# Rounding two of five stored parts into tiles of the results' pool

## The chip, the cores and the metric

The kernel runs on one core of one Trainium2 chip, as one launch. The metric is the device time of one execution, in microseconds (us). Before the change three executions took 2423.63, 2425.55 and 2424.79 us; the median is 2424.79 us. A measurement of this kernel can tell a difference of about 0.2% (some 4.8 us) from none.

## The reference, cut to what matters

One layer of a decoder on 512 tokens of width 2048, all in float32:

```
h = rmsnorm(x, g_mix);  z = h @ w_in            # conv, attention and gate columns
merged = gc * (conv_y @ w_conv_out) + ga * (attn @ w_attn_out)
x = x + merged @ w_mix_out                       # the mixing projection
h = rmsnorm(x, g_mlp)                            # the second norm
u = square(relu(h @ w_ff1));  x = x + u @ w_ff2  # the MLP
out = rmsnorm(x, g_final)
```

The change touches the rows between the mixing projection and the first MLP product: the projection's results, transposed and scaled, are combined into the sums that the MLP's first product reads.

## The kernel before, in words

**Products.** Every large product is done by Winograd's form of Strassen's scheme: a 2x2 block product with seven products instead of eight, named A11, A12, S1, S2, S3, S4 and A22 after the combination of the left operand that they use. `Group` does one such set of seven for 512 columns of weights. Each weight quarter is a 1 MB tile `x`, loaded by a transfer on SP's queue. Since TensorE works in a rounded float32 here, each operand is split in two: ScalarE (ACT) rounds it into `th` (`high_of`, line 111) and VectorE (DVE) subtracts that to get the rest, `tl` (`low_of`, line 114). A product is then three passes over the same PSUM bank: high by high, high by low, low by high. `th` and `tl` have two buffers each, so a split can start only when TensorE has done with the `th` of two products earlier. In the mixing projection one product is 48 matmuls (`mm_rows`, lines 187, 189 and 191: 16 with `th` and 8 with `tl` for each of two blocks of tokens).

**The mixing projection** is four groups, g = 0 to 3. For each group, `Mix(g)` takes the four result blocks (`put`, line 1266: adds the residual x and stores to `x1_d`). `turn` squares them for the norm (line 524), transposes them on TensorE (line 1283, into `ptr`) and copies the transposes into two tiles `f` (line 1292). Then `sums` makes the five combinations S1, S2, S3, S4 and A22 that the MLP's left operand needs, and `out` splits each in high and low and sends both to `h_d` in HBM by a transfer from GpSimd's (POOL's) queue. This is done for g = 0, 1 and 2, each during the next group's products; A11 and A12 are kept unsplit in `f_d`. Group 3 keeps its parts in the core's memory. After the last group the stored parts are read back (`begin_part`, line 1241).

**The last group** uses `tail3`. Its order of products is A11, A12, S1, S2, S4, S3, A22. The bank `a` holds A11 + S2, is copied and read three times, and is then overwritten by A22. While it runs, the MLP's first group `g0` starts: its weights are loaded from POOL's queue (`x<-in_w_ff`), the stored half of A11 and A12 is split (`split_part`), and its products A11 and A12 follow A22 on TensorE.

**Tiles.** The results of the groups (`o`), the residual rows (`xr`) and a few others come from one tag with five places of 128x512 float32 (`otile`). The rounded parts come from `staged`, a tag with two places. A place is handed out again when everything that reads the old tile is done, the transfer that stores it included. A rounding into a `staged` tile thus waits for the landing of the store of the part two before it.

**Order.** The order on each engine is made by the layer that records the program: it plans with its own estimates, and moves work ahead where it believes another would wait. It is fixed when the program is built; on the chip each engine works through its list strictly in order, so an instruction that waits holds all behind it. `split_in_order` pins the part splits in the order of the program on ACT and DVE.

Of the kernel before, what the change touches and what calls it, by code (L numbers as in the profile page):

```python
# [9 lines left out]
F32R = mybir.dt.float32r  # L10
# [5 lines left out]
P = 128  # L16
# [4 lines left out]
HS = S // 2  # L21
# [23 lines left out]
@with_exitstack  # L45
def tile_hybrid_block(ctx: ExitStack, tc, x, g_mix, w_in, b_f, b_gate, conv_w, w_conv_out,
                      w_attn_out, w_mix_out, g_mlp, w_ff1, w_ff2, g_final, out):
    nc = tc.nc
    x, out = x[0], out[0]
# [20 lines left out]
    def otile(shape, name, dt=F32):  # L70
        return main.tile(shape, dt, tag="o", name=name, bufs=5)
# [44 lines left out]
    def split(src, hi, lo):  # L116
        return high_of(src, hi), low_of(src, hi, lo)
# [3 lines left out]
    def split_in_order(*how, kept=None):  # L121

        for i in split(*how):
            tc.keep_in_program_order(i)
            parted[kept] = i

    def sub(out, a, b):
        return nc.vector.tensor_tensor(out=out, in0=a, in1=b, op=ALU.subtract)  # L128
# [841 lines left out]
    n = 0  # L970
# [244 lines left out]
    def staged():  # L1215
        return pm.tile([P, 2, HS], F32R, tag="staged", name="staged", bufs=2)
# [7 lines left out]
    n = turns[0] + 1  # L1224
# [24 lines left out]
    class Mix:  # L1249
# [50 lines left out]
        def out(self, n, src):  # L1300
            g = self.g
            if self.last:
                split(src, Q2[n][:, 0, 2 * g:], Q2[n][:, 1, 2 * g:])
            else:
                hi = staged()
                split_in_order(src, hi, src)
                for e, o in enumerate((hi.bitcast(F32), src)):
                    nc.gpsimd.dma_start(out=h_d[:, SPLIT.index(n), e, 2 * g:2 * g + 2], in_=o)
# [424 lines left out]
```

## Time and profile before

| | |
|---|---|
| three executions | 2423.63, 2425.55, 2424.79 us |
| span of the profiled execution | 2423.6 us, mean granted TensorE clock 0.998 |
| TensorE (PE) busy | 2401.9 us (99%) |
| VectorE busy | 2041.3 us (84%) |
| ScalarE busy | 1202.6 us (50%) |
| mixing projection's products | to 1188 us; the third group begins near 1106, the last near 1146 us |
| MLP's first product | from about 1188 us |

The profile gives times from the start of the span. In a timeline row stand the start, the duration, the engine, the line, the operation with output and input (buffer numbers left out), shapes, and in brackets the idle time of the engine before it with what ended it. A matmul's duration includes the drain of the pipeline; the distance of two starts is what it costs. The row of a window gives its length, then for PE, PE's weight loads, DVE, ACT and POOL the busy time and, in brackets, the number of instructions, then the granted clock, the share of the transfer engines and GB/s. In a row of transfers the last number is the time from issue to landing.

### The profile page before, as it was taken

The page shows a single profiled execution, that of the slowest core. Times are in us where ns is not written, and L with a number is a line of the kernel's source. Part 1 is how long each engine was busy: PE and PEld are TensorE (multiplying, and loading weights), DVE is VectorE, ACT ScalarE, POOL GpSimd, SP SyncE. Part 2 cuts the span into 40 slices and gives each one's busy share as a digit, 9 for nine tenths or more (in the row PEclk, how much of TensorE's full clock was granted, in tenths as well). Part 3 has the DMA queues.
Part 4 walks back from the last instruction along what each step waited for, and adds up shares of the span by engine and source line. Part 5 has one row for each costly group of instructions (what it writes and reads, how often), then busy time and mean ns, then how long its engine had stood idle before and what let it go on. Part 6 is the DMA issues. An engine that isn't in the chain of part 4 may idle for free.

```text
span 2423.6 us, 41438 instructions
## 1 busy us (share of the span) xinstructions
PE 2401.9 (99%) x17783; PEld 2260.7 (93%) x17783; DVE 2041.3 (84%) x1739; ACT 1202.6 (50%) x1230; POOL 299.9 (12%) x480
## 2 busy tenths in 40 slices
PE   9999999999999999999999999999999999999998
PEld 9999899999999999899999999999998888888886
DVE  7887677788887878898989889898887888889898
ACT  7443434445545534355666566666664333333334
POOL 1110111111111111022300000000011001100000
PEclk9999999999999999999999999999999999999999
DMA  8665454464656755657855564655678567665662
GB/s 276 188 187 153 148 157 140 144 189 152 201 187 199 239 179 187 209 169 243 315 201 207 198 232 177 231 192 200 229 296 291 166 217 251 217 206 184 235 229 101
DMA packets 279847, 491.98 MB, mean 203 GB/s; under 512 B 11820, under 2 KB 191112, under 8 KB 279280
## 3 DMA queue, kind: packets, MB, share of 16 engines
q1 hardware_dynamic: 226384, 272.71, 35.7%
q0 software_dynamic: 52672, 215.57, 24.3%
q8 instruction: 139, 2.28, 0.4%
q10 hardware_dynamic: 608, 1.06, 0.1%
q14 instruction: 44, 0.36, 0.0%
HBM read 379.70 MB, written 109.07 MB: 202 GB/s over the span
## 4 chain that ended last, share of the span: by engine, by line
PE 86%; DVE 4%; issue 4%; DMA 3%; ACT 1%; POOL 1%; SPq 0%; DVEq 0%; POOLq 0%; ACTq 0%
PE a L168 6%; PE a L172 6%; PE a L170 6%; PE a L189 5%; PE a L187 5%; PE a L191 5%; PE d L168 5%; PE d L170 5%; PE d L172 5%; PE c L168 4%; PE c L170 4%; PE c L172 4%; PE d L191 3%; PE d L189 3%; PE d L187 3%
## 5 line engine op out<-in xcount | busy, mean ns | idle before, releaser
L111 ACT ACTIVATE th<-x 128x2048 fp32r<-128x2048 f32 (+1 forms) x280 | 537.0, 1918 | 503.7 <-DVE x L128 159.2
L114 DVE TENSOR_TENSOR tl<-x,th 128x2048 fp32r<-128x2048 f32 (+2 forms) x282 | 639.4, 2273 | 162.1 <-ACT th L111 150.5
L128 DVE TENSOR_TENSOR x<-x,x 128x2048 f32<-128x2048 f32 (+1 forms) x160 | 366.0, 2288 | 24.4 <-DMA x<-in_w_in_dram 18.9
L111 ACT ACTIVATE th<-y 128x2048 fp32r<-128x2048 f32 (+1 forms) x109 | 185.4, 1701 | 273.9 <-PE a L189 138.8
L114 DVE TENSOR_TENSOR tl<-y,th 128x2048 fp32r<-128x2048 f32 (+1 forms) x109 | 219.0, 2014 | 29.3 <-ACT th L111 28.9
L187 PE MATMUL a<-th,us 128*128 128x512 f32 x512 | 199.3, 389 | 0.4 <-ACT th L111 0.4
L189 PE MATMUL a<-th,us 128*128 128x512 f32 x512 | 199.2, 389 | 0.0
L170 PE MATMUL c<-S,th 128*128 128x256 f32 x848 | 196.4, 277 | 0.0
L168 PE MATMUL c<-S,th 128*128 128x256 f32 x848 | 196.3, 277 | 0.0
L168 PE MATMUL a<-S,th 128*128 128x256 f32 x784 | 181.1, 277 | 0.0
L170 PE MATMUL a<-S,th 128*128 128x256 f32 x784 | 180.7, 276 | 0.0
L170 PEld LDWEIGHTS c<-S,th 128*128 128x128 f32 x848 | 159.3, 188 | 0.2 <-issue 0.2
L168 PEld LDWEIGHTS c<-S,th 128*128 128x128 f32 x848 | 159.4, 188 | 0.0
L170 PEld LDWEIGHTS a<-S,th 128*128 128x128 f32 x784 | 147.3, 188 | 0.0
L168 PEld LDWEIGHTS a<-S,th 128*128 128x128 f32 x784 | 147.2, 188 | 0.0
L191 PE MATMUL a<-tl,us 128*128 128x512 f32 x512 | 136.9, 389 | 0.6 <-DVE tl L114 0.6
L170 PE MATMUL b<-A,th 128*128 128x256 f32 x544 | 127.3, 279 | 0.0
L168 PE MATMUL a<-A,th 128*128 128x256 f32 x544 | 126.7, 278 | 0.0
L168 PE MATMUL d<-S,th 128*128 128x256 f32 x544 | 126.1, 277 | 0.0
L170 PE MATMUL a<-A,th 128*128 128x256 f32 x544 | 126.0, 277 | 0.0
L168 PE MATMUL b<-A,th 128*128 128x256 f32 x544 | 126.0, 276 | 0.0
L170 PE MATMUL d<-S,th 128*128 128x256 f32 x544 | 125.7, 277 | 0.0
(398 smaller groups left out, 6065.2 us busy)
## 6 DMA issues: line engine op xcount, KB each, us to landing
x<-in_w_in_dram SPq DMA_DIRECT2D x86, 1024.0 KB, 6.0
y<-in_w_ff_dram SPq DMA_DIRECT2D x64, 1024.0 KB, 7.7
x<-in_w_ff_dram SPq DMA_DIRECT2D x60, 1024.0 KB, 8.6
us<-s_d POOLq DMA_DIRECT2D x48, 1024.0 KB, 9.3
s_d<-rh POOLq DMA_DIRECT2D x32, 896.0 KB, 5.2
s_d<-r POOLq DMA_DIRECT2D x32, 896.0 KB, 6.0
x<-in_w_mix_out_dram SPq DMA_DIRECT2D x17, 1024.0 KB, 6.7
g_d<-o POOLq DMA_DIRECT2D x32, 256.0 KB, 3.1
```

The lines of the kernel that those rows point to most:

```text
L111: return tied(nc.scalar.activation(out=hi, in_=src, func=AF.Copy))
L114: return tied(nc.vector.tensor_tensor(out=lo, in0=src, in1=hi.bitcast(F32), op=ALU.subtract))
L128: return nc.vector.tensor_tensor(out=out, in0=a, in1=b, op=ALU.subtract)
L168: nc.tensor.matmul(o, hi[:, q, js], Sh, start=first and q == 0 and j == 0, stop=False, skip_group_check=True)
L170: nc.tensor.matmul(o, hi[:, q, js], Sl, start=False, stop=False, skip_group_check=True)
L172: nc.tensor.matmul(o, lo[:, q, js], Sh, start=False, stop=q == nq - 1, skip_group_check=True)
L187: tied(nc.tensor.matmul(o, Sh, hi[:, q, :], start=begin and q == 0, stop=False, skip_group_check=True))
L189: tied(nc.tensor.matmul(o, Sl, hi[:, q, :], start=False, stop=False, skip_group_check=True))
L191: tied(nc.tensor.matmul(o, Sh, lo[:, q, :], start=False, stop=q == nq - 1, skip_group_check=True))
```

## The change

In `Mix.out`, for the parts S1 and A22, the rounded half goes into a tile `hi` of the results' tag (five places) and no longer into one of the two `staged` tiles. S2, S4 and S3 stay with `staged`. Nothing is added or removed: the same roundings, subtractions and stores are done, with the same shapes.

```
-                hi = staged()
+                hi = otile([P, 2, HS], "hi", F32R) if n in ("S1", "A22") else staged()
```

A group now takes eight tiles of the five-place tag, not six. In the built program the places fall as follows (numbers are the program's own). In the second group `hi_11634` (S1) takes the place of `o_11346`, and `hi_11832` (A22) that of `o_11406`, both results of the first group; `o_11840` then follows `hi_11634`, and `o_11897` follows `hi_11832`. In the last group `hi_12764` (A22) lies where the result block `o_12827` has to go; before the change `o_12827` followed `o_12555`.

The planner's order moves with it. The first piece is ACT's in the second group, - before and + with the change. `th_11902` is the high half of the weights of that group's last product, A22; `staged` and `hi` are roundings of parts of group 0; `o_11777` is the copy of the bank of S3.

```order
 L111 ACTIVATE th_11845<-x11_11650 128x2048
 L111 ACTIVATE staged_11629<-f_11031 128x512
-L111 ACTIVATE staged_11634<-s1_11619 128x512
+L111 ACTIVATE hi_11634<-s1_11619 128x512
+L111 ACTIVATE staged_11706<-f_11032 128x512
 L260 ACTIVATE o_11777<-d_11712 128x512
-L111 ACTIVATE staged_11706<-f_11032 128x512
-L111 ACTIVATE staged_11832<-f_11032 128x512
+L111 ACTIVATE hi_11832<-f_11032 128x512
 L111 ACTIVATE th_11902<-x10_11538 128x2048
```

S1 and A22 go into `hi`, S3's rounding moves ahead of the copy, and the third and fourth rounding no longer share places with the two before them.

The second piece is ACT's in the last group, from the MLP's first half splits on. `th_12891` belongs to A22 of the mixing projection, `th_12981` to A11 of the MLP, `o_12770` and `o_12827` are the copies of the banks of S2 and S4; `A11_12615` is the stored half of the MLP's A11.

```order
+L1288 ACTIVATE A12_12684<-ptr_12753,cols_97 128x256
+L111 ACTIVATE th_12891<-x10_12461 128x2048
+L1292 ACTIVATE f_12455<-ptr_12753,cols_97 128x256 x2
+L111 ACTIVATE hi_12764<-f_11969 128x512
 L260 ACTIVATE o_12770<-a_12463 128x512
 L111 ACTIVATE A11_12615<-A11_12615 128x1536
-L1288 ACTIVATE A12_12684<-ptr_12753,cols_97 128x256
-L1292 ACTIVATE f_12455<-ptr_12753,cols_97 128x256 x2
-L111 ACTIVATE staged_12764<-f_11969 128x512
+L111 ACTIVATE th_12981<-x00_12822 128x2048
 L260 ACTIVATE o_12827<-c_12629 128x512
-L111 ACTIVATE th_12891<-x10_12461 128x2048
```

The copy `o_12827` now stands behind `th_12981`, and the split of the mixing projection's A22 ahead of the copies. On DVE the addition of bank `a` to `o_12827` (`o_12827<-a_12463`), the last reader of that bank before A22 overwrites it, moved from ahead of `tl_12892` to behind `tl_12982`, the low half that goes with `th_12981`.

The third piece is TensorE's in the last group: the end of S3 (`d_12832`), then A22 of the mixing projection (`a_12463`), its transposes, and A11 of the MLP (`a_12980`). The change's order, without its further rows of the same kind:

```order
 L191 MATMUL d_12832<-tl_12834,M_10785 128x256 x2
 L191 MATMUL d_12832<-tl_12834,M_10986 128x256 x2
+L168 MATMUL a_12980<-A11_12615,th_12981 128x256
+L170 MATMUL a_12980<-A11_12615,th_12981 128x256
...
 L187 MATMUL a_12463<-th_12891,M_10539 128x256
 L189 MATMUL a_12463<-th_12891,M_10539 128x256
...
 L1283 MATMUL ptr_12962<-ident_90,o_12692 128x128 x4
-L168 MATMUL a_12980<-A11_12615,th_12981 128x256
-L170 MATMUL a_12980<-A11_12615,th_12981 128x256
```

28 of the 48 matmuls of the MLP's A11 moved from behind the mixing projection's A22 to ahead of it.

## The prediction

> **What bounds the kernel now.** The page first: engine shares and the chain that ended last.
>
> ```profile
> PE 2401.9 (99%) x17783; PEld 2260.7 (93%) x17783; DVE 2041.3 (84%) x1739; ACT 1202.6 (50%) x1230; POOL 299.9 (12%) x480
> PE 86%; DVE 4%; issue 4%; DMA 3%; ACT 1%; POOL 1%; SPq 0%; DVEq 0%; POOLq 0%; ACTq 0%
> ```
>
> TensorE is busy for 99% of the span, so an edit to roundings on ACT can only be worth what TensorE waits near them. Next, windows over the mixing projection and PE's waits from 1030 to 1230 us:
>
> ```profile
> 1080.00:1100.00 20.00, 17.33 (x143) 16.93 (x142) 12.99 (x12) 10.13 (x13) 6.13 (x11) 0.96 0.90 296
> 1160.00:1180.00 20.00, 18.80 (x166) 18.61 (x165) 18.16 (x20) 14.93 (x23) 9.43 (x16) 1.00 0.81 282
> PE d L187 <- ACT th L111: 2.5, 1, 2.5
> PE c L187 <- ACT o L260: 1.2, 1, 1.2
> ```
>
> Two waits, 2.5 us in the second group and 1.2 us in the last, are all that TensorE loses there, and the first costs it speed as well. The ACT timeline shows what the first comes from, the PE timeline and 1 us windows what it costs:
>
> ```profile
> 1083.27 0.57 POOL L1308 DMA_DIRECT2D h_d<-staged  x1 [6.84 <-ACT staged L111]
> 1086.08 0.63 ACT L111 ACTIVATE staged<-s 128x512 fp32r<-128x512 f32 x1 [0.30 <-DMA h_d<-staged]
> 1094.90 0.63 ACT L111 ACTIVATE staged<-f 128x512 fp32r<-128x512 f32 x1 [7.71 <-DMA h_d<-staged]
> 1096.28 1.89 ACT L111 ACTIVATE th<-x 128x2048 fp32r<-128x2048 f32 x1
> 1098.22 0.58 PE L187 MATMUL d<-th,M 128*128 128x256 f32 x1 [2.53 <-ACT th L111]
> 1105.52 0.60 PE L1283 MATMUL ptr<-ident,o 128*128 128x128 f32 x4
> 1111.41 0.82 PE L1283 MATMUL ptr<-ident,o 128*128 128x128 f32 x6
> 1099.00:1100.00 1.00, 1.00 (x7) 1.00 (x6) 1.00 (x1) 1.00 (x2) 0.00 (x0) 0.50 0.97 377
> 1100.00:1101.00 1.00, 1.00 (x7) 1.00 (x7) 1.00 (x2) 1.00 (x1) 0.00 (x0) 0.50 0.23 90
> ```
>
> ACT stands 7.71 us before a rounding into `staged`, since the store that empties the tile has not landed; behind it queues `th` of A22, and TensorE waits for that. After the wait the granted clock is 0.50, and the pass takes 1105.52 - 1098.22 = 7.30 us; the next takes 1111.41 - 1105.52 less 0.44 for four transposes = 5.45 us. The slow clock costs 1.85 us. The 1.2 us wait leaves the clock at 1.00 and comes from ACT's order (a split and a rounding ahead of a copy), which the change leaves alike.
>
> **The change, part by part.** The work is the same; only places and order move.
>
> *Second group: the 2.5 us wait goes.* S2 and S4 take the two `staged` tiles, S1 a place whose old content was stored a group earlier. S3 follows S2, whose store was issued at 1083.27 and landed 2.7 us later, by the first row below. S4's, issued at 1086.7, took 8.1 us, and that is what ACT waits for now; A22 takes a free place too.
>
> ```profile
> h_d<-staged POOLq DMA_DIRECT2D x1, 256.0 KB, 2.7
> h_d<-staged POOLq DMA_DIRECT2D x1, 256.0 KB, 8.1
> h_d<-f POOLq DMA_DIRECT2D x1, 256.0 KB, 8.4
> 1088.76 1.07 PE L191 MATMUL a<-tl,M 128*128 128x256 f32 x8
> ```
>
> From 1086.0 ACT runs S1, S3, a copy and A22 without a stop to about 1088.0; `th` can start when TensorE has read its buffer's old content (1088.76), and is done near 1090.8, with 4.7 us to spare. What is late next: the copies of the next transposes into `f` (L1292) overwrite a tile whose last store is issued near 1089.0 and took 8.4 us, so they start at 1097.4 and hold up `th` of the third group's first product: 1097.4 + 0.8 + 0.6 + 0.4 + 1.9 = 1101.1. TensorE needs it at 1095.53 + 5.45 + 0.44 = 1101.4. That just holds. **Term A: -2.5 - 1.85 = -4.4 us**; between 0 and -4.4.
>
> *Third group.* Here ACT now does the two copies into `f` and a rounding ahead of `th` of S2, which before came first:
>
> ```profile
> 1125.84 1.93 ACT L111 ACTIVATE th<-x 128x2048 fp32r<-128x2048 f32 x1 [4.15 <-DVE x L128]
> 1127.88 0.84 ACT L1292 ACTIVATE f<-ptr,cols 128x256 f32<-128x256 f32 x2
> 1129.52 0.28 PE L187 MATMUL a<-th,M 128*128 128x256 f32 x1
> h_d<-f POOLq DMA_DIRECT2D x1, 256.0 KB, 4.5
> ```
>
> The copies wait for a store that is issued near 1122.7. If it takes 4.5 us as before, `th` ends at 1127.2 + 0.7 + 0.5 + 1.9 = 1130.3, 0.8 us late; if it takes 2.7 us, `th` ends by 1128.5 and nothing is late. The queue has less in it, so I take nearer the lower end. **Term B: +0.3 us**, between 0 and 0.8.
>
> *Last group: a new wait.* The rows that carry it (PE, ACT, DVE timelines, and the store of A22's rounding, issued at 1177.6):
>
> ```profile
> 1175.62 1.07 PE L191 MATMUL c<-tl,M 128*128 128x256 f32 x8
> 1181.06 1.07 PE L191 MATMUL d<-tl,M 128*128 128x256 f32 x8
> 1181.97 0.28 PE L187 MATMUL a<-th,M 128*128 128x256 f32 x1
> 1183.78 1.07 PE L191 MATMUL a<-tl,M 128*128 128x256 f32 x8
> 1187.01 1.11 PE L191 MATMUL a<-tl,M 128*128 128x256 f32 x8
> 1181.26 1.92 ACT L111 ACTIVATE th<-x 128x2048 fp32r<-128x2048 f32 x1 [0.66 <-PE d L189]
> 1187.21 1.92 ACT L111 ACTIVATE th<-x 128x2048 fp32r<-128x2048 f32 x1
> 1191.26 1.50 ACT L111 ACTIVATE A<-A 128x1536 fp32r<-128x1536 f32 x1
> 1178.11 0.69 DVE L131 TENSOR_TENSOR o<-a,o 128x512 f32<-128x512 f32 x1
> 1192.79 1.76 DVE L114 TENSOR_TENSOR A<-A 128x1536 fp32r<-128x1536 f32 x1 [1.01 <-ACT A L111]
> 1202.07 2.29 DVE L114 TENSOR_TENSOR tl<-x,th 128x2048 fp32r<-128x2048 f32 x1
> 1204.41 2.15 PE L172 MATMUL c<-S,tl 128*128 128x256 f32 x16
> h_d<-staged POOLq DMA_DIRECT2D x1, 256.0 KB, 7.0
> ```
>
> Step 1. After S3's product (its end is the start of the next, 1181.97) TensorE now has 28 matmuls of the MLP's A11. Their `th` is the ACT row at 1181.26; it cannot start before TensorE leaves the same buffer in that S3 product ([0.66 <-PE d]). Done at 1183.2: TensorE waits 1.25 us. Step 2. 16 such matmuls take 1183.78 - 1181.97 = 1.81 us, so 28 take 3.2, to 1186.4. Step 3. A22 then overwrites bank `a`, which DVE must have added to `o_12827` first. That addition ran at 1178.11 and was never near the path. Now ACT's copy that fills `o_12827` waits for `hi_12764`'s store: `th` of A22 can start near 1175.8, then two copies, so the rounding ends near 1179.0; the store lands 7.0 us after, near 1186.0, and the copy is done at 1186.6. On DVE the addition stands behind `tl` of the MLP (2.3 us). That one's turn comes after the subtraction for A22's part, an addition, the low half of A11 (1181.2 to 1182.9, after ACT's high half) and three additions of 0.6 us: 1184.7 to 1186.9. So the addition ends at 1187.6 by either wait. **A22 starts at 1187.65, not 1181.97: 5.7 us later**, 3.2 us of it filled with work brought forward.
>
> Step 4. That work does not come back as a gain. Behind A22's last read of its `th` (1187.01) stands a chain: `th` of the MLP's A12 (1187.21), small copies, the high half of the stored A12 (1191.26), its low half on DVE (1192.79 to 1194.5), then TensorE's A12. TensorE covers it now with A11's 48 matmuls and two sets of transposes. With 28 of them done before, what remains behind A22 is 0.44 + 4 x 0.11 + 1.8 + 0.44 = 3.1 us; the chain still takes 6.6. It slides by the whole 5.7 us, and A12 starts at 1200.15 after a wait of 3.4 us. The DVE chain behind it slides as well (row 1202.07, for which TensorE waits at 1204.41 now). Step 5. A wait of 2.5 us took the clock to 0.50, at a cost of 1.85 us, so one of 3.4 us should: A12 5.45 + 1.85, a small matmul and S1's first 32 matmuls (3.6) end near 1211.2, against DVE's 1204.36 + 5.7 = 1210.05: 1.1 us more. **Term C: +5.7 + 1.1 = +6.8 us.** Its lower bound is 0 (the addition in time, the order harmless), its upper 10: the store takes 10.6 us, as one there did (below), and the chain slides by 3.3 more.
>
> ```profile
> x_d<-o POOLq DMA_DIRECT2D x1, 256.0 KB, 10.6
> ```
>
> The Trainium skill puts this otherwise: its page "TensorE: Matmul & The Clock Gate", section "Part 1: The HAM clock gate", has the clock halved after at least one whole idle window of about 3.4 us. By that rule the 2.5 us wait should have left the clock alone, and this trace differs; a 3.4 us wait would be a toss-up, and without the slow clock the sum would be 1.1 us lower, which the forecast's width holds.
>
> The weight loads of the MLP are issued earlier or at the same time; the read-back of the stored parts follows the last result's store, some 5 us later, but has 10 us and more until its product.
>
> *Sum.* -4.4 + 0.3 + 6.8 = +2.7 us: 2423.6 becomes 2426.3 us in a profiled execution. That one is 1.2 us under the median of the runs, so on the median of 2424.79 I expect **2427.4 us**. Measurement tells 0.2%, 4.85 us, from no change; this is inside.
>
> **The rivals.**
>
> *The wait goes and nothing takes its place.* Term A alone, with C near 0 or 1: 2420.4 to 2421.5 us. For it: A is the largest wait in these stages, and DVE and ACT are not full. Against: the rule that a result follows A22's rounding in its place, and the order in which TensorE meets A11's matmuls first, do not depend on luck. Even in full it stays just under the 4.85 us that counts as faster; it passes that if the 1.2 us wait shrinks too (2419.2).
>
> *Late stores decide, and it is slower.* `o_12827`'s place: if `hi_12764`'s store lands later than 7.3 us after its issue it takes the lead from DVE in step 3, and each us more is a us on the end. At 10.6 us the sum is +6 and the time 2430.8. It sits behind three 1 MB weight loads in POOL's queue, one of which now starts earlier; against it, the store before took 7.0 us in much the same queue.
>
> *The stall moves by one product and does nothing else.* If `f`'s store in term A lands 3 us later, `th` of the third group is late by that, the slow clock returns, and A shrinks to nothing: with C, 2431.9 us. The margin is only 0.4 us, but a delay of 0.5 to 2 us would merely cost its own length.
>
> **How the numbers follow.** My forecast, with steps within 2 to 3 us, has 0.68; the clean gain 0.12; late stores or a stall that moves 0.20. From the first nearly all lies within 0.2% (2420 to 2429.6); of the second a little under half is beyond it, of the third most. That makes 0.06 faster, 0.75 the same, 0.19 slower. The range: the forecast with C 4 us smaller at one end, and late stores at the other, 2422.6 to 2431.0.
>
> **What would show it.** Step A: no wait of PE for `th` near 1095 us, the clock at 1.00 from 1098 to 1102, ACT's roundings of the second group without an idle time over 1 us. Term C: PE idle near 1178 (1182 less 4.4) for `th`, again about 3 us of matmuls later until DVE's `o<-a`, then some 3 us for `A<-A`, with a clock of 0.50 after it. If A22 of the last group starts straight after S3 or A11's 28, or ACT's copy `o_12827` never waits for `h_d<-hi`, step 3 is wrong and the time is that of the first rival; if PE waits at the third group's first product, the margin in A was.

## The result, and the profile after

The changed kernel takes 2432.5 us (median of 7 executions, 2432.0 to 2437.3) against 2425.55 us of the kernel before on the same chip (7 executions, 2421.8 to 2427.2): a ratio of 1.0036 with a 95% interval of 1.0026 to 1.0045. It is slower, by 7 us, where 2.6 us were forecast. The profiled executions differ by 2431.4 - 2423.6 = 7.8 us. Two executions far outside the rest, 9210.5 us of e11 and 4930.7 us of e12, are left out of the ratios below.

The shares of the engines and the chain that ended last, in the page of the changed kernel, say almost nothing: TensorE is as full as before.

```profile
PE 2405.3 (99%) x17783; PEld 2263.2 (93%) x17783; DVE 2041.8 (84%) x1739; ACT 1201.7 (49%) x1230; POOL 299.9 (12%) x480
```

```profile
PE 90%; DVE 3%; issue 3%; DMA 2%; POOL 1%; ACT 1%; SPq 0%; DVEq 0%; POOLq 0%; ACTq 0%
```

TensorE's waits do (waiting engine, tile and line, what it waited for; us in all, times, longest):

```profile
PE ptr L1283 <- DVE o L1266: 3.0, 2, 2.5
PE a L187 <- ACT th L111: 2.2, 1, 2.2
PE b L161 <- ACT A L111: 1.5, 1, 1.5
PE b L170 <- DVE A L114: 1.3, 1, 1.3
PE a L168 <- ACT th L111: 1.1, 1, 1.1
PE c L187 <- ACT o L260: 0.9, 1, 0.9
PE a L187 <- DVE o L131: 0.6, 1, 0.6
PE c L187 <- DVE o L131: 0.5, 1, 0.5
```

The 2.5 us wait for `th` in the second group is gone. In its place stand a wait of transposes for residual additions (3.0), one for an addition to a result (0.5), four in the last group (1.1, 0.6, 1.5, 1.3), and one of 2.2 us that turns out to lie far behind, in the MLP. The wait of 1.2 us for ScalarE's copy is now 0.9. To see where the time went, the same instructions of both kernels are set side by side. TensorE's timeline of the changed kernel, with one row of VectorE's from the MLP:

```profile
1088.06 1.07 PE L191 MATMUL a<-tl,M 128*128 128x256 f32 x8
1089.64 0.39 PE L187 MATMUL c<-th,M 128*128 128x256 f32 x1 [0.51 <-DVE o L131]
1101.06 0.60 PE L1283 MATMUL ptr<-ident,o 128*128 128x128 f32 x4
1107.35 0.60 PE L1283 MATMUL ptr<-ident,o 128*128 128x128 f32 x4
1110.40 0.66 PE L1283 MATMUL ptr<-ident,o 128*128 128x128 f32 x4 [2.45 <-DVE o L1266]
1122.96 0.63 PE L1283 MATMUL ptr<-ident,o 128*128 128x128 f32 x4 [0.60 <-DVE o L1266]
1128.88 0.28 PE L187 MATMUL a<-th,M 128*128 128x256 f32 x1
1802.41 2.29 DVE L114 TENSOR_TENSOR tl<-y,th 128x2048 fp32r<-128x2048 f32 x1 [3.15 <-ACT th L111]
1820.75 0.50 PE L187 MATMUL a<-th,us 128*128 128x512 f32 x1 [2.16 <-ACT th L111]
```

The rows of the kernel before that belong to the last two (the others stand in the prediction):

```profile
1796.54 2.29 DVE L114 TENSOR_TENSOR tl<-y,th 128x2048 fp32r<-128x2048 f32 x1 [3.15 <-ACT th L111]
1813.07 0.50 PE L187 MATMUL a<-th,us 128*128 128x512 f32 x1 [0.37 <-ACT th L111]
```

| place | before | after | difference | change since the row above | forecast |
|---|---|---|---|---|---|
| second group, S2's last low pass | 1088.76 | 1088.06 | -0.70 | scatter before the change acts | 0 |
| transposes behind A22 | 1105.52 | 1101.06 | -4.46 | **-3.8** | -4.4 |
| third group, S2 begins | 1129.52 | 1128.88 | -0.64 | **+3.8** | +0.3 |
| MLP, the same low half | 1796.54 | 1802.41 | +5.87 | **+6.5** | +6.8 |
| end of the span | 2423.6 | 2431.4 | +7.8 | +1.9 | 0 |

So the gain came, 3.8 us of it, and was given back in full within 28 us. The cost in the last group came near the forecast. The last 1.9 us lie at 1820 us, where the change moves nothing: the wait of 2.16 us and a half clock behind it, against three waits of 0.4 to 0.6 us in the kernel before.

**The last group** as rows: TensorE's four waits, and ScalarE's copy that waits for its place.

```profile
1183.13 0.38 PE L168 MATMUL a<-A,th 128*128 128x256 f32 x1 [1.11 <-ACT th L111]
1187.22 0.38 PE L187 MATMUL a<-th,M 128*128 128x256 f32 x1 [0.63 <-DVE o L131]
1198.18 0.36 PE L161 MATMUL b<-A,th 128*128 128x192 f32 x1 [1.52 <-ACT A L111]
1199.97 0.39 PE L170 MATMUL b<-A,th 128*128 128x256 f32 x1 [1.30 <-DVE A L114]
1185.70 0.60 ACT L260 ACTIVATE o<-c 128x512 f32<-128x512 f32 x1 [2.62 <-DMA h_d<-hi]
```

A wait of 1.1 us for the MLP's `th`, the 28 matmuls of its A11, a wait of 0.6 us for the addition of bank `a`, and A22 at 1187.22; then 2.8 us for the split of the stored A12. The copy that holds the addition waits for A22's stored rounding, as step 3 said.

**The third group**: why the transposes wait. ScalarE's and VectorE's rows after:

```profile
1096.09 0.84 ACT L1292 ACTIVATE f<-ptr,cols 128x256 f32<-128x256 f32 x2 [5.92 <-DMA h_d<-f]
1099.32 1.90 ACT L111 ACTIVATE th<-x 128x2048 fp32r<-128x2048 f32 x1
1101.25 2.29 DVE L114 TENSOR_TENSOR tl<-x,th 128x2048 fp32r<-128x2048 f32 x1 [2.38 <-PE d L191]
1109.66 0.69 DVE L1266 TENSOR_TENSOR o<-o,xr 128x512 f32<-128x512 f32 x1
```

and the same three steps before, with TensorE's transposes:

```profile
1099.27 1.93 ACT L111 ACTIVATE th<-x 128x2048 fp32r<-128x2048 f32 x1
1101.74 2.28 DVE L114 TENSOR_TENSOR tl<-x,th 128x2048 fp32r<-128x2048 f32 x1
1110.15 0.68 DVE L1266 TENSOR_TENSOR o<-o,xr 128x512 f32<-128x512 f32 x1
1111.41 1.03 PE L1283 MATMUL ptr<-ident,o 128*128 128x128 f32 x8
```

VectorE's share of that stretch before (window, length, then busy time of TensorE, of its weight loads, of VectorE; the third number from the right is the granted clock):

```profile
1101.00:1130.00 29.00, 29.00 (x250) 29.00 (x250) 28.69 (x24) 18.43 (x37) 9.89 (x16) 0.99 0.61 195
```

This is the key to the result. TensorE came 4.5 us earlier, but `th` of the third group's first product did not (1099.32 against 1099.27): it stood behind the two copies into `f`, which wait for a store until 1096.09, and behind what follows them in ScalarE's list (the copy of bank `a`, and a square of the result that VectorE makes of it). VectorE's work on it starts at 1101.25 against 1101.74. (The bracket of that row names TensorE's low pass, which ended at 1101.22 together with `th`. In e1, e3, e6 and e12 the row starts at the end of `th` while that pass still runs, so it is `th` that counts.) From there VectorE has something to do without a gap, 28.7 of 29 us in the kernel before. The last residual addition of the second group comes 8.4 us down that list, at 1109.66 against 1110.15, and the transposes need it. Before, TensorE reached eight of them at 1111.41; the first four belong to an earlier result (in the changed kernel they run at 1107.35 without a wait), and at 0.11 us each the four that need this addition started at 1111.85. The addition had ended at 1110.15 + 0.68 = 1110.83. There was about 1.0 us to be gained, not 4.4. Counted from start to start, the waits at 1110.40 and 1122.96 cost 2.6 and 0.8 us of the 3.8; most of the rest went at 1103.60, where A11's low pass starts 0.06 us behind the end of its low half (1101.25 + 2.29 = 1103.54).

### The profile page after: what moved, and what is told of

It reads as the page before. It is cut to its first block, busy times and chain, and to the rows that moved or that the text cites. A ratio compares the mean times of both kernels' runs of the same rounds, so it can differ in the third digit from the quotient of the medians.

```text
span 2431.4 us, 41436 instructions
## 1 busy us (share of the span) xinstructions
PE 2405.3 (99%) x17783; PEld 2263.2 (93%) x17783; DVE 2041.8 (84%) x1739; ACT 1201.7 (49%) x1230; POOL 299.9 (12%) x480
## 4 chain that ended last, share of the span: by engine, by line
PE 90%; DVE 3%; issue 3%; DMA 2%; POOL 1%; ACT 1%; SPq 0%; DVEq 0%; POOLq 0%; ACTq 0%
PE a L172 6%; PE a L168 6%; PE a L170 6%; PE d L172 5%; PE d L168 5%; PE d L170 5%; PE a L191 5%; PE a L187 5%; PE a L189 5%; PE c L168 4%; PE c L170 4%; PE c L172 4%; PE d L189 3%; PE d L187 3%; PE d L191 3%
```

## The experiments

My theory: the gain is lost because VectorE's list in the third group does not start earlier, and the last group costs its own 6.5 us. Rivals: the parts of the last group disturb what lies ahead of them; the places of the results, or the weights, are late; or VectorE simply has too much to do there.

The profiles are compared by the time of one and the same matmul in both (the nth of the program, TensorE's order being the same or nearly so), from 1080 us on, less the difference that is there at 1080. That removes what differs before. Between 1240 and 1280 us some profiles, one of the unchanged kernel among them, run 1.3 to 1.4 us longer; so I read at 1220 us, although the expectations say 1300.

### Which group does what

**e1**, groups 0 and 1 only; **e2**, group 2 only; **e3**, group 0 only:

```
-                hi = staged()
+                hi = otile([P, 2, HS], "hi", F32R) if g < 2 and n in ("S1", "A22") else staged()     # e1
+                hi = otile([P, 2, HS], "hi", F32R) if g == 2 and n in ("S1", "A22") else staged()    # e2
+                hi = otile([P, 2, HS], "hi", F32R) if g == 0 and n in ("S1", "A22") else staged()    # e3
```

> The change for the parts of the first two groups only (g < 2); the part of group 2, stored during the last group, stays in staged. Theory 1 (TensorE's gain of 4.4 us in the second group is lost in the third, because VectorE's list there starts behind the same th as before, at 1099.3 us, so the transposes wait for additions; and the last group costs its own 6.5 us): waits of 0.5 at 1090, 2.4 at 1110 and 0.6 us at 1123 as in the full change, none in the last group but the old one of about 1 us, span 0.6 us below before (-0.4 to -1.5). Rival (the parts of the last group change the order of what comes before it, and without them the gain stays): span 3.5 to 4.4 us below before, no wait of 2.4 us at 1110.

> The change for the part stored during the last group only (g = 2). Theory 1: waits of 2.5 us with the half clock in the second group as before, and in the last group 1.1 + 0.6 + 1.5 + 1.3 us with a half clock after them: span 6.5 us above before (6 to 7). Rival (the waits of the last group come from TensorE arriving there earlier, not from the place that the result takes): less than 3 us above before.

> The change for the parts of group 0 only, those stored during the second group. Theory 1: the wait of 2.5 us and its half clock go (4.4 us), 0.5 and 2.4 us come back at 1090 and 1110, the third group is as before, so about 1.4 us below before remain (0.5 to 1.6). If instead the third group's own change made the wait at 1110 (rival), it is gone here and 3.5 to 4.4 us remain.

| | ratio of the times, 95% interval | 1080 to 1220 us |
|---|---|---|
| e1, groups 0 and 1 | 1.0012 [1.0003, 1.0021] | +1.0 us |
| e2, group 2 | 1.0024 [1.0015, 1.0033] | +5.6 us |
| e3, group 0 | 1.0011 [1.0002, 1.0019] | -1.3 us |

The cost sits in the last group: e2 alone has the four waits of the changed kernel to within 0.25 us, in TensorE's timeline:

```profile
1182.89 0.39 PE L168 MATMUL a<-A,th 128*128 128x256 f32 x1 [1.15 <-ACT th L111]
1187.21 0.38 PE L187 MATMUL a<-th,M 128*128 128x256 f32 x1 [0.86 <-DVE o L131]
1198.16 0.35 PE L161 MATMUL b<-A,th 128*128 128x192 f32 x1 [1.44 <-ACT A L111]
1199.95 0.38 PE L170 MATMUL b<-A,th 128*128 128x256 f32 x1 [1.30 <-DVE A L114]
```

It came to 5.6 us and not 6.5; no half clock follows here. And the gain does not stay when the last group is left out: e1 and e3 have the wait at the transposes all the same, so that rival is out. In TensorE's timeline, e1's row:

```profile
1109.83 0.66 PE L1283 MATMUL ptr<-ident,o 128*128 128x128 f32 x4 [2.22 <-DVE o L1266]
```

and e3's:

```profile
1109.07 0.66 PE L1283 MATMUL ptr<-ident,o 128*128 128x128 f32 x4 [2.33 <-DVE o L1266]
```

In e1 a half clock follows the wait, in e3 none, which is most of what parts them. The runs of e1 and e3 are slower than before by 0.5 to 5 us, while e3's profile is ahead: one profile is one execution, and half clocks fall in some and not in others (below).

### The same kernels again

**e5** is the kernel before, **e6** is e3, **e8** the changed kernel, with no edit.

> The kernel before, unchanged, once more: what the comparison makes of no change, and a second profile of it. Expected: a ratio whose interval holds 1, the wait of 2.5 us and its half clock in the second group again, and other waits at about 1815 us (in the MLP, where a weight transfer took 12.6 to 15.8 us in the five profiles so far and TensorE waited 0 to 2.2 us) if those are scatter of the transfers, the same 0.4 + 0.6 + 0.6 us if they belong to the kernel.

> The kernel of e3_one_group once more. From 1080 to 1300 us its profile was 1.4 us ahead of before's, by the clock of each matmul; its runs were 2 us behind. Theory 1: the profile shows the same 1.4 us between 1080 and 1300 us (within 0.3, or 1.7 us less if the half clock falls after the wait of 2.3 us this time), and what differs else lies before 400 us and at 1815 us, where the change moves nothing. Rival (the change costs time elsewhere): a difference at a third place, the same in both profiles.

> The changed kernel once more, on the same chip as e5 to e7: waits of 0.5, 2.4 and 0.6 us in the second and third group and 1.1 + 0.6 + 1.5 + 1.3 us in the last as before, 6 to 7 us behind the kernel before between 1080 and 1300 us, and at 1815 us another wait than 2.2 us if that one is scatter.

| | ratio, 95% interval | 1080 to 1220 us | wait at the transposes | half clock after it | wait for `th` at 1820 us |
|---|---|---|---|---|---|
| e5, before | 1.0000 [0.9991, 1.0009] | -0.1 us | none | - | none (before: 0.37) |
| e6, as e3 | 1.0013 [1.0004, 1.0022] | +0.6 us | 2.22 | yes | 0.99 (e3: 1.7) |
| e8, the change | 1.0032 [1.0020, 1.0045] | +9.6 us | 2.32 | yes | 0.37 (after: 2.16) |

e6 is 1.8 us behind e3 with the same waits: that is one half clock of 3.41 us. So the change for group 0 gains nothing on the mean of executions, which is what the runs say. The wait at 1820 us is scatter: the changed kernel has 2.16 us once and 0.37 once. It follows a weight transfer there that took 17.1 us in the one and 15.3 us in the other (from issue to landing 13.8 to 17.1 us in all profiles; the expectation of e5 has figures more than 1 us lower). e8 pays 9.6 us because two half clocks follow the waits of the last group and one the transposes.

### Taking the additions out of the way

**e7**: as e3, and VectorE's sum of the weight quarters in the third group is ordered behind the last residual addition.

```
-            if not self.pinned:
-                sub(X[0, 0], X[0, 1], X[0, 0])
+            with tc.issue_after(self.behind.added.ins) if self.behind else ExitStack():
+                self.pinned or sub(X[0, 0], X[0, 1], X[0, 0])
...
+        group = groups[g]; group.behind = mixes[1] if g == 2 else None
```

> As e3_one_group, and on VectorE the additions of the residual to the second group's last two results are put ahead of the sum of the weight quarters and of the low half that stood ahead of them in the third group. Theory 1 (the transposes wait for additions that stand behind 4.6 us of other work on VectorE): the wait of 2.3 us at 1109 us goes, and from 1080 to 1300 us the kernel is 3.5 to 4 us ahead of before, unless a low half is late at the third group's third product. Rival (the residual rows or the results' places are late): the wait stays above 1.5 us.

The ratio is 1.0006 [0.9997, 1.0015]; from 1080 to 1220 us -0.1 us, where a lead of 3.5 to 4 us was expected. VectorE's rows show the additions ahead of the second low half, and TensorE's the waits that are left:

```profile
1104.16 2.29 DVE L114 TENSOR_TENSOR tl<-x,th 128x2048 fp32r<-128x2048 f32 x1 [2.39 <-ACT th L111]
1108.42 0.69 DVE L1266 TENSOR_TENSOR o<-o,xr 128x512 f32<-128x512 f32 x1
1129.83 0.39 PE L187 MATMUL a<-th,M 128*128 128x256 f32 x1 [1.12 <-ACT th L111]
1132.83 1.18 PE L191 MATMUL a<-tl,M 128*128 128x256 f32 x8 [0.90 <-DVE tl L114]
```

The wait at the transposes is gone; at 1125 us the kernel is 3.3 us ahead. Then S2's high and low half are late and the rest goes as well: what was put behind the additions, the sums of weight quarters first, is needed 20 us later. The edit orders VectorE's work and leaves the places and the weights as in e3, so those rivals are out for the wait. The theory holds for the wait and not for the 3.5 us that should have stayed.

**e4**: as e3, and the transposes one product later.

```
-        late = g == 1
+        late = g in (1, 2)
```

> As e3_one_group, and the transposes of the second group's last two results, with the sums behind them, are put one product later in the third group (behind A12 and not A11). Theory 1: the additions, done by 1110.4 us, are no longer waited for at 1108, the wait of 2.4 us is gone, and 3.5 to 4.4 us below before remain if nothing else is late there. Rival (the weights set the pace: the transfer engines are at 100% from 1088 to 1100 us and th or tl comes late all the same): the wait reappears at a later product of the third group, and no more than 1.5 us below before remain.

The ratio is 1.0018 [1.0009, 1.0026]; from 1080 to 1220 us +0.7 us. At 1130 us it was 3.7 us ahead. The sums now come late, and the old illness returns one group on: ScalarE waits for a store before it can round into `staged`.

```profile
1135.68 1.39 ACT L111 ACTIVATE staged<-f 128x512 fp32r<-128x512 f32 x2 [5.90 <-DMA h_d<-staged]
```

### Starting VectorE's list earlier

**e9**: as e3, and the transposes of the second group's first result are made behind A11 of the third group, so that the copies into `f` no longer stand ahead of `th`. **e10**: the same with groups 0 and 1. **e11**: the kernel before with this move alone.

```
-        for n in ("A12", "S3") if late else ("A11", "S2" if g == 3 else "S1"):
+        for n in ("A12",) if late else ("A11", "S2" if g == 3 else "S1"):
```

> As e3_one_group, and the transposes of the second group's first result are made together with the other three behind A11 of the third group, so that ScalarE's two copies into f, which wait for a store until 1096.1 us, no longer stand ahead of the high half of the third group's first weights. Theory 1 (VectorE is full from 1101 to 1130 us, 28.7 of 29 us, and begins there no earlier than before because that high half waits behind the copies): the high half starts near 1094 and VectorE's work on it near 1096 and not 1101, the wait of 2.3 us is gone, and from 1080 to 1300 us the kernel is 3 to 4 us ahead of before. Rival (VectorE's own amount of work is the bound there, wherever it begins): waits for th or tl come at 1125 to 1140 us as in e7_additions_first and no more than 1 us is left.

> As e9_copies_later, with the change for the parts of groups 0 and 1. Theory 1: as e9, 3 to 4 us ahead of before from 1080 to 1300 us, and no rounding that waits for a staged store in the third group. Rival (the results' places are too few): the residual rows of the third group land late, an addition waits for them, and less than 2 us is left.

> The kernel before, with only the move of the transposes of e9_copies_later: all five parts stay in staged. Theory 1: th of A22 no longer stands behind the rounding that waits for a store (the order has that rounding behind it now), so the 2.5 us wait and its half clock go as well; VectorE starts its work in the third group as late as that rounding lets it, near 1098 us: 1 to 4 us ahead of before from 1080 to 1300 us. Rival (it was the place that counted): the wait of 2.5 us stays and the kernel is within 1 us of before.

| | ratio, 95% interval | 1080 to 1220 us |
|---|---|---|
| e9 | 1.0018 [1.0009, 1.0027] | +3.4 us |
| e10 | 1.0013 [1.0004, 1.0022] | +0.7 us |
| e11 | 1.0003 [0.9994, 1.0012] | +1.3 us |

e9 missed by 7 us, and e10 and e11 by 2 us and more. ScalarE shows why in e9:

```profile
1100.50 0.60 ACT L260 ACTIVATE o<-a 128x512 f32<-128x512 f32 x1 [8.70 <-DMA h_d<-hi]
1100.99 1.91 ACT L111 ACTIVATE th<-x 128x2048 fp32r<-128x2048 f32 x1
```

With the copies out of the way the next instruction in the list is the copy of bank `a` into a result tile, and that tile's place holds a rounded part whose store lands at 1100.5. Behind the store of `f` stood the store of `hi`: the change has made the results wait for the parts. So `th` came later than before, not earlier. In e11 the parts stay in `staged`, TensorE's wait for A22's `th` shrinks from 2.5 to 1.68 us with no half clock, the transposes wait 0.24 us and S2's high half makes TensorE wait 0.98 us at 1127.21, and the time is the same. e10 waits 2.01 us at the transposes and 0.85 us for S2's high half.

**e12**: as e3, without the four stores of group 0's S1 and S3 in the second group. Their place in `h_d` is filled some 45 us earlier from another tile, by four stores added at line 1267, which are not shown here; so this kernel leaves out that part of the computation.

```
-                for e, o in enumerate((hi.bitcast(F32), src)):
+                for e, o in () if g == 0 and n in ("S1", "S3") else enumerate((hi.bitcast(F32), src)):
```

> As e3_one_group, but the four stores of the first group's S1 and S3 to HBM are left out of the second group, where the transfer engines are at 100% (that region is filled from another tile some 30 us earlier, so the parts read back later are not the right ones: this kernel leaves that part of the computation out). Theory 1, as e9 left it (ScalarE's and VectorE's lists in the third group begin when the stores of the second group have landed): 1 MB less in the queue lets the copies into f start 2 to 3 us earlier than 1096.1, VectorE's work on the third group's first low half starts by 1099 and not 1101.2, the wait of 2.3 us at 1109 shrinks below 0.5, and from 1080 to 1300 us the kernel is 3 to 4 us ahead of before. Rival (VectorE has too much to do in the third group, whenever it begins, or the high half waits for something else): the low half starts at 1101 again or waits of 2 us or more come later in the third group, and no more than 1.5 us is left.

The ratio is 1.0011 [1.0002, 1.0021]; +0.6 us from 1080 to 1220. The copies into `f` start at 1095.05, which by TensorE's own progress (its lead or lag at 1080 us taken off) is 0.1 us later than in e3, on which this is built; the wait at the transposes is 2.46 us. The lever moved nothing: three of the four stores that were left out stand behind the one that counts, and the 4 MB of weights beside it stay. So e12 says nothing for or against the theory.

**e13**: as e3, with that one store on another queue.

```
-                    nc.gpsimd.dma_start(out=h_d[:, SPLIT.index(n), e, 2 * g:2 * g + 2], in_=o)
+                    (nc.scalar if g == 0 and n == "S4" and e else nc.gpsimd).dma_start(out=h_d[:, SPLIT.index(n), e, 2 * g:2 * g + 2], in_=o)
```

> As e3_one_group, with one store of the second group, that of S4's low half (the one that the copies into f wait for until 1096.1 us), sent from ScalarE's queue and not from GpSimd's, where it lands behind five others. Theory 1 (the wait of 2.3 us for the additions is the end of a chain that starts where that store lands: copies into f, copy of bank a, high half, low half, sums, additions, 14.3 us in all, with nothing idle on VectorE behind the high half): the store lands 2 us or more earlier, every step of the chain comes earlier by as much, the wait shrinks to 0.3 us or less, and from 1080 to 1300 us the kernel is 3 to 4 us ahead of before. Rival (VectorE's third group is bound by something else, or too full): the low half starts at 1101 us all the same, or the time comes back as waits for th or additions from 1120 to 1140 us; 1.5 us or less is left.

The ratio is 1.0004 [0.9994, 1.0013]; -1.1 us from 1080 to 1220. ScalarE, VectorE and TensorE:

```profile
1094.55 0.84 ACT L1292 ACTIVATE f<-ptr,cols 128x256 f32<-128x256 f32 x2 [2.96 <-DMA h_d<-f]
1097.45 0.60 ACT L260 ACTIVATE o<-a 128x512 f32<-128x512 f32 x1 [2.06 <-DMA h_d<-hi]
1099.89 2.29 DVE L114 TENSOR_TENSOR tl<-x,th 128x2048 fp32r<-128x2048 f32 x1 [0.40 <-ACT th L111]
1109.04 0.66 PE L1283 MATMUL ptr<-ident,o 128*128 128x128 f32 x4 [1.18 <-DVE o L1266]
```

By TensorE's progress the copies start 1.1 us earlier than in e3, on which this is built, and 2.0 us earlier than in the changed kernel. Then the copy of bank `a` waits 2.06 us for the store of `hi`; the low half starts 0.9 us earlier than in e3, at 1099.89, and the wait goes from 2.33 to 1.18 us. This is the dose that the theory wants: less delay, less wait. The lead of 3 to 4 us that was expected did not come. Set over all kernels in which TensorE waits at that place, the link is exact.

| | third group's first low half starts | the transposes start | difference | TensorE waited |
|---|---|---|---|---|
| after | 1101.25 | 1110.40 | 9.15 | 2.45 |
| e1 | 1100.68 | 1109.83 | 9.15 | 2.22 |
| e3 | 1099.92 | 1109.07 | 9.15 | 2.33 |
| e6 | 1101.83 | 1110.98 | 9.15 | 2.22 |
| e8 | 1100.70 | 1109.85 | 9.15 | 2.32 |
| e9 | 1102.93 | 1112.08 | 9.15 | 1.89 |
| e10 | 1100.14 | 1109.30 | 9.16 | 2.01 |
| e11 | 1099.11 | 1108.26 | 9.15 | 0.24 |
| e12 | 1100.21 | 1109.37 | 9.16 | 2.46 |
| e13 | 1099.89 | 1109.04 | 9.15 | 1.18 |

Whenever TensorE arrives, the transposes start 9.15 us after that low half; its wait is just the rest. (The kernel before: 1101.74 + 9.15 = 1110.89, and TensorE came to these four at 1111.85.)

**e14**: e13 and e7 together.

> e13_other_queue and e7_additions_first together: group 0's S1 and A22 in the results' tag, S4's low half stored from ScalarE's queue, and VectorE's additions ahead of the sum and the low half in the third group. Theory 1: the third group's first low half starts near 1099.9 as in e13, the additions are done 5 us later as in e7 and not 9.1, TensorE waits neither for them nor for the high halves at 1104 and 1130 us (in e7 1.6 us in all, with a start 2 us later), so from 1080 to 1220 us the kernel is 3 to 4 us ahead of before, and its runs 2 to 4 us faster than before's. Rival (VectorE has too much work from 1101 to 1130 us): the additions are in time, but high or low halves are waited for between 1120 and 1140 us, 1 us or less is left, and the runs are the same.

The ratio is 1.0002 [0.9993, 1.0011]; +0.7 us from 1080 to 1220. Neither the transposes nor anything else is waited for until 1125 us, where the kernel is 4 us ahead of where it was at 1090. TensorE's next rows:

```profile
1125.93 0.39 PE L187 MATMUL a<-th,M 128*128 128x256 f32 x1 [0.39 <-ACT th L111]
1128.93 1.20 PE L191 MATMUL a<-tl,M 128*128 128x256 f32 x8 [0.89 <-DVE tl L114]
```

VectorE's share of 1101 to 1130 us there, as above:

```profile
1101.00:1130.00 29.00, 27.71 (x235) 27.31 (x234) 27.64 (x25) 18.78 (x32) 10.07 (x17) 1.00 0.54 177
```

S2's halves are late again and 2.6 us go. A wait of 1.3 us for an addition at 1089.6, which comes from VectorE's order in this kernel, takes most of the rest. The rival holds here: with the low half starting 1.1 us earlier than in the kernel before by TensorE's progress (1099.07 against 1101.74 on the clock, of which 1.6 us are a lead that was there at 1080) and the additions in time, VectorE's work still isn't done when TensorE needs it at 1129.

## Why the prediction was wrong, point by point

**Term A, second group (-4.4): the gain was right, its keeping was wrong.** The wait for `th` and its half clock went, ScalarE's roundings run from 1084.2 to 1087.0 without a gap, and the copies into `f` start at 1096.09, where 1097.4 was worked out. Of 4.4 us, 3.8 came; 0.5 us went to an addition for which TensorE waits at 1089.64 and which I had not looked at. The step that failed is "What is late next". It followed one line from those copies, to the `th` that TensorE needs next, found it in time by 0.3 us, and stopped: "That just holds". It did hold. But the same `th` is also the head of VectorE's list, and 8.4 us down that list stand the additions for the next transposes. The trace of before had the rows (1110.15, ended 1110.83, against the transposes that need it at 1111.85): a margin of 1.0 us. e7 shows that these additions are the wait, e13 and the table that its length is set by when that list starts.

**Term B, third group (+0.3, between 0 and 0.8).** Apart from the 2.45 us that belong to A, TensorE lost 0.60 us there, inside the bounds, but for an addition (1122.96) and not for `th` of S2, which was in time.

**Term C, last group (+6.8).** Steps 1 to 4 came as written: 1.11 us for `th` (forecast 1.25), A22 held by the addition of bank `a` behind the copy that waits for the stored `hi`, 6.7 us from issue to landing (forecast 7.0), the MLP's A12 behind a wait of 2.8 us (forecast 3.4). A22 starts 5.25 us later than before (1187.22 against 1181.97); TensorE was 0.15 us ahead at S3's last pass (1180.91 against 1181.06), so 5.4 us against the 5.7 of the forecast. The whole came to 6.5 us in the changed kernel's first profile, of which 0.5 went ahead of that pass, so that 6.0 belong to the term; 5.6 in e2, more in e8. Step 5, the slow clock, is a matter of luck in its size: none in e2, one half clock in the first profile, two in e8.

**The sum.** 2.7 us were forecast for the profile and 7.8 found: 3.5 of the difference is the gain given back in the third group, 0.6 a smaller gain, 1.9 the scatter at 1820 us, less 0.7 from before the change acts and 0.3 in C. The range ended at 2431.0. (Its lower end, 2422.6, does not follow from "C 4 us smaller", which gives 2427.4 - 4 = 2423.4; nothing here hangs on that.) The rival "the stall moves by one product" has nearly the measured time (2431.9), but not the mechanism: it wanted `th` late and a half clock, and `th` was in time.

**The size of the doubt.** I gave the clean gain 0.12 and "slower" 0.19. All that had been weighed for A was one deadline; the margin of 0.3 us there should have been a warning to look for the next one.

**What stays open.** Thirteen profiles of the eleven versions that remove or shrink the wait in the second group stand between 1.9 us ahead and 2.9 us behind at 1150 us, and no version is faster than before in its runs. That VectorE's list is what they meet is shown for the transposes, and by e7 and e14 for S2's halves. Whether a different order of VectorE's whole third group would keep part of the 4 us was not tried. No version here beats the kernel before; e7, e11, e13 and e14 can't be told from it.

## What to carry to other kernels

A wait of the busiest engine is worth only what the next full engine leaves of it: before costing its removal, find the instruction that the waiting engine needs next from each other engine, and read from the trace how long ahead of it that one is done; the least of these margins bounds the gain as long as that engine does not start earlier too (here 1.0 of 4.4 us). An engine that is busy for 28.7 of 29 us behind a late start can be the bound there even if nobody waits for it yet. And tiles that wait for stores should not share places with tiles that the main chain fills: the results then wait for the stores.

## What the runs showed of the hardware

**The clock is decided in fixed windows of 3.41 us.** Every stretch of half clock in these profiles, but for the one in which each execution ends, is 3.413 us long, or twice that, and all of them in one execution begin on one grid: in the changed kernel they begin at 1200.98 and 1822.20 us, 621.2 us apart, which is 182.0 windows; in e12 at 1108.94 and 1815.50, 207.0 windows. The half clock at the end begins on the same grid, so it gives the grid where there is no other. With it each wait can be put into its windows. In sixteen profiles, all twelve windows in which TensorE was idle for 1.80 us or more were followed by one at half clock, and no full-speed window with 1.77 us or less was (1.71 us in e3 and 1.77 us in e9, at the transposes, are the longest). One with 1.01 us idle was, but it ran at half clock itself. So the line lies at about half the window, and a wait of 2.2 to 2.5 us is followed by a half clock, which costs another 1.7 us (half of 3.41), or by none, by where it falls. The changed kernel's wait of 2.45 us at 1110 was cut by a window's edge into 0.87 and 1.58 us, and no half clock followed; e1's of 2.22 us lay in one window. In windows of 2 us, the stretch behind the wait in the changed kernel:

```profile
1110.00:1112.00 2.00, 1.60 (x14) 1.60 (x15) 2.00 (x2) 1.91 (x8) 1.35 (x3) 1.00 0.29 111
1112.00:1114.00 2.00, 2.00 (x20) 2.00 (x19) 2.00 (x2) 0.82 (x2) 1.19 (x2) 1.00 0.93 334
```

and in e1:

```profile
1110.00:1112.00 2.00, 2.00 (x13) 2.00 (x13) 2.00 (x2) 1.91 (x8) 1.92 (x4) 0.62 0.34 115
1112.00:1114.00 2.00, 2.00 (x12) 2.00 (x12) 2.00 (x1) 0.24 (x1) 0.62 (x1) 0.53 0.79 285
```

The Trainium skill, "TensorE: Matmul & The Clock Gate", section "Part 1: The HAM clock gate", has a free-running window of 3413 ns, which these profiles agree with, and halves the clock after at least one idle window, which they don't: here a window idle for half its length was enough.

**TensorE's pace differs by up to 4% at a granted clock of 1.00.** Between 1240 and 1280 us a window of 20 us holds 172 or 173 matmuls in five profiles, the unchanged kernel's second among them, and 176 to 179 in the rest, but for e13, which has 174 in its first half and 179 in its second. No wait goes with it in those five, and no run here tells its cause.

**One transfer in a full stretch scatters by 3 us.** The last weight transfer ahead of 1800 us, issued at the same point of the program every time, took 13.8 to 17.1 us in the sixteen profiles, and TensorE's wait for what comes of it goes with that: none up to 14.9 us, 0.37 at 15.3, 0.9 to 1.0 at 15.8 and 15.9, 2.1 to 2.2 at 17.0 and 17.1. In the changed kernel:

```profile
y<-in_w_ff_dram SPq DMA_DIRECT2D x1, 1024.0 KB, 17.1
```

That alone is 2 us between executions of one kernel, and up to 1.7 more where a half clock follows.
